# Score maxima as float16 pairs before the transpose, and value sums that start with a product instead of a zero matmul: one layer kernel on Trainium2

## Chip, cores and metric

One core of a Trainium2 chip. The metric is the device time in microseconds of one execution of the whole kernel; the number compared is the median of several executions. The kernel before has a median of 2942.72 us in 3 runs (2941.49 to 2947.78).

## The reference

One transformer layer over 2048 latent tokens (width 1024) with 256 context tokens: a modulated RMS norm, one input projection, a bidirectional chunked retention (4 heads), a grouped-query attention (8 query heads of 64, 2 key heads, 256 + 2048 keys), an output projection and a squared-ReLU MLP. The change sits in the attention:

```python
def _dense_attention(q, k, v):
    s = jnp.einsum('bqkgd,bskd->bkgqs', q, k).astype(jnp.float32) * ATT_SCALE
    p = jax.nn.softmax(s, axis=-1).astype(v.dtype)
    return jnp.einsum('bkgqs,bskd->bqkgd', p, v)
```

Everything is float32 in the reference. The kernel reaches that with pairs of float16: a `hi` part (the value cast down) and a `lo` part (what the cast lost).

## The kernel before

The kernel runs in three stages one behind another: projections (up to about 655 us), attention with retention and output projection beside it (about 655 to 1660 us), and the MLP (to the end).

**Groups and steps.** The attention is cut into 32 *groups*, one for each of 16 tiles of 128 queries and 2 key heads; a group holds 4 query heads, so 512 query columns. There are NK = 18 tiles of 128 keys. A table of events, `on(k, phase, fn)`, says which function issues its instructions in step k; within a step the phases run in the order `begin, scores, piece, maximum, early, exp, cast, low, chain, pe, values, late, dma`. `chain` is a list from which one entry is taken after the phases maximum, low and late. The order that results is the program order of each engine; no engine reorders. A group takes 18 steps, and a group's maxima are computed beside the exponentials of the group before.

**Maxima (lines 160 to 196).** For each group, 18 `piece` matmuls (L165, L169) give scores with the query on the partitions, in PSUM tiles `mp`, of which there are two buffers; `maximum` (L178, VectorE) reduces each piece to a negated maximum in `nm`. `least` (L184) takes the minimum over a head's five numbers and writes it twice, by two reductions, into columns 64 and 96 of a float32 tile `mt` (column 80 holds a constant). `turn` (L189, TensorE) transposes `mt` by four float32 matmuls with the identity, into a PSUM tile that is the next `mp` buffer. `rows` (L192, ScalarE) copies rows 64 to 127 of it, divided by 8192, into the float16 query tile `qr`, and `rows2` (L196, VectorE) overwrites rows 96 to 127 with what that cast lost. So the maxima become extra rows of the queries, and the score matmuls (L202, L203) subtract them.

**Exponentials and values.** `exp` (L208, ScalarE) writes float32 probabilities, `cast` (L212, ScalarE) their float16 `phi`, `low` their `plo`, on GpSimd (L219) for five of nine pairs of key tiles and on VectorE (L221) for the others. `values` (L223 to 236) adds, for each pair of key tiles, 16 products into two PSUM tiles `o`: a `plo` product (65 columns wide) and a `phi` product (129 columns) for each of 2 key tiles and 4 heads. Two heads share one `o` tile. Ahead of a group's first pair, two matmuls of a zero tile with 258 columns (L227) open the sums of the two tiles with `start=True`.

**Beside it.** Retention (L1083 to 1155), the output projection (L1259 to 1281) and the norm ahead of the MLP (L1288 to 1316) are spread over the same steps and use all engines; L1233, L1226 and L1231 prepare output weights in the first groups.

Of the kernel before, what the change touches and what calls it, by code (L numbers as in the profile page):

```python
# [11 lines left out]
F32 = mybir.dt.float32  # L12
F32R = mybir.dt.float32r
F16 = mybir.dt.float16
BF16 = mybir.dt.bfloat16
I32 = mybir.dt.int32
AF = mybir.ActivationFunctionType
ALU = mybir.AluOpType
AX = mybir.AxisListType
# [3 lines left out]
P = 128  # L23
# [6 lines left out]
NK = NT + NC  # L30
H = 4
CH = 128
HD = 64
# [3 lines left out]
PSHIFT = 8  # L37

ROW = 8192.0
VW = 2 * HD + 1  # L40
# [14 lines left out]
def layer_kernel(ctx: ExitStack, tc: tile.TileContext, a: dict, out: bass.AP):  # L55
    nc = tc.nc
    mm = nc.tensor.matmul

    const = ctx.enter_context(tc.tile_pool(name="const", bufs=1, reuse_waits="tile"))
    dram = ctx.enter_context(tc.tile_pool(name="dram", bufs=1, space=DRAM))  # L60

    ident = const.tile([P, P], F32, name="ident")
    make_identity(nc, ident)

    def split(hi, lo, src, eng=None):
        nc.scalar.activation(hi, src, AF.Copy)
# [67 lines left out]
    wv = kp.tile([P, 2, NK, VW + 1], F16, name="wv")  # L134
# [6 lines left out]
    class Group:  # L141
# [36 lines left out]
            nc.vector.tensor_reduce(dst, src, axis=AX.X, op=ALU.max, negate=True)  # L178

        def least(self, mt):  # L180
            self.mt = mt
            nm = self.nm.rearrange("p a b c -> p (a b) c")
            for c in (64, 96):
                nc.vector.tensor_reduce(mt[:, :, c], nm, axis=AX.X, op=ALU.min)  # L184

        def turn(self):
            self.m = psS.tile([P, 4, P], F32, name="mp", tag="mp")
            for h in range(4):
                nc.tensor.transpose(self.m[:, h], self.mt[:, h], ident)  # L189

        def rows(self):
            nc.scalar.activation(self.qr[64:, 1], self.m[64:], AF.Copy, scale=1 / ROW)  # L192

        def rows2(self):
            lo = self.qr[96:, 1]
            nc.vector.scalar_tensor_tensor(lo, self.m[96:], 1 / ROW, lo, op0=ALU.mult, op1=ALU.subtract)  # L196

        def scores(self, kt):
            ps = self.s[kt] = psS.tile([P, 512], F32, name="st", tag="st")
# [23 lines left out]
        def values(self, j):  # L223
            if j == 0:
                self.o = [psV.tile([P, 2, VW], F32, name=f"o{b}", tag=f"o{b}") for b in range(2)]
                for o in self.o:
                    mm(o, zeros, wv[:, 0, :2, :VW], start=True, stop=False)  # L227
            hi, lo = self.hi.pop(j), self.lo.pop(j)
            for i in range(2):
                v = wv[:, self.g, 2 * j + i]  # L230
                for h in range(4):
                    o = self.o[h // 2][:, h % 2]
                    c = slice(h * P, (h + 1) * P)
                    last = 2 * j + i == NK - 1 and h % 2 == 1
                    mm(o[:, : HD + 1], lo[:, i, c], v[:, : HD + 1], start=False, stop=False)  # L235
                    mm(o, hi[:, i, c], v[:, :VW], start=False, stop=last)  # L236

        def evacuate(self):
            self.so = op.tile([P, 4, VW], F32, name="so", tag="so")
# [20 lines left out]
    with ExitStack() as st:  # L260
# [5 lines left out]
        op = st.enter_context(tc.tile_pool(name="op", bufs=2, reuse_waits="tile"))  # L266
        sm = st.enter_context(tc.tile_pool(name="sm", bufs=3, reuse_waits="tile"))
# [623 lines left out]
        for n, (g, c) in enumerate(todo):  # L891
# [7 lines left out]
            last = c == len(PLAN[g]) - 1  # L899
# [10 lines left out]
            for m, (kind, i) in enumerate(GROUPS[g]):  # L910
                if not (kind == "c" and col in (C_RQ, C_RG, C_AQ)):
                    ps, k = (begun.pop(m), 6) if n == 0 and m in begun else (None, 4)
# [40 lines left out]
    op = pool(attn, "op2", 2)  # L953
# [13 lines left out]
    nc.vector.tensor_tensor(unit, ident[:, 64:65], ident[:, 96:97], op=ALU.add)  # L967
    nc.vector.tensor_tensor(unit, unit, ident[:, 80:81], op=ALU.add)
    nc.vector.tensor_scalar_mul(unit, unit, ROW)
    zeros = vp.tile([P, P], F16, name="zeros")  # L970
    nc.vector.memset(zeros, 0.0)
    mts = [vp.tile([P, 4, P], F32, name=f"mt{i}") for i in range(2)]
    for mt in mts:
        nc.gpsimd.memset(mt, 0.0)

        nc.gpsimd.memset(mt[:, :, 80], PSHIFT * math.log(2.0) * HD**0.5)

    def more_keys(g, i):
        s = slice(i * 768, (i + 1) * 768)
# [8 lines left out]
    def on(k, phase, fn, *args):  # L988
        events.setdefault((k, phase), []).append((fn, args))
# [28 lines left out]
    def attention():  # L1018
        for n, g in enumerate(groups):
            k = NK * n  # L1020
            if n > 0:
                on(k - 14, "dma", g.load)
                on(k - 1, "late", g.minima, sm)
                for i in range(NK):
                    on(k + i, "piece", g.piece, i)
                    on(k + i + 1, "maximum", g.maximum, i)
            else:
                on(k + NK, "begin", g.load)
            on(k + NK, "chain", g.least, mts[n % 2])
            on(k + NK + 1, "piece", g.turn)  # L1030
            on(k + NK + 2, "cast", g.rows)
            on(k + NK + 3, "early", g.rows2)
            k += LAG
            for i in range(NK):
                on(k + i, "scores", g.scores, i)
                on(k + i + 1, "exp", g.exp, i)
            for j in range(NK // 2):
                on(k + 2 * j + 3, "cast", g.cast, j)
                if j in POOL_PAIRS:
                    on(k + 2 * j + 4, "low", g.low, j)  # L1040
                else:
                    for i in range(2):
                        on(k + 2 * j + 4 + i, "low", g.low, j, i)
                on(k + 2 * j + 6, "values", g.values, j)
            k += NK + 5
            on(k, "cast", g.evacuate)
            on(k + 1, "chain", g.invert)
            on(k + 2, "late", g.combine, ats)
        return NK * len(groups) + LAG + 8
# [758 lines left out]
```

## Time and profile before

| | |
|---|---|
| median of 3 runs | 2942.72 us (2941.49 to 2947.78) |
| the profiled execution's own time | 2946.76 us |
| its span, first to last instruction | 2945.0 us |
| granted TensorE clock, mean | 0.987 |
| TensorE / VectorE / ScalarE / GpSimd busy | 94% / 74% / 47% / 53% of the span |
| first and last transposition of maxima (L189) | 678.2 and 1604.3 us |

In the profile PE is TensorE's matmuls, PEld its weight loads, DVE is VectorE, ACT ScalarE, POOL GpSimd, SP the queue that issues DMAs. A matmul's end is modelled: matmuls overlap, so a matmul's cost to the queue is read from the distance between the starts of two neighbours, not from its duration. The same holds in small for DVE, where an instruction may start a little ahead of the end of the one before. A wait is put down to what came last.

### The profile page before, as it was taken

The page shows a single profiled execution, that of the slowest core. Times are in us where ns is not written, and L with a number is a line of the kernel's source. Part 1 is how long each engine was busy: PE and PEld are TensorE (multiplying, and loading weights), DVE is VectorE, ACT ScalarE, POOL GpSimd, SP SyncE. Part 2 cuts the span into 40 slices and gives each one's busy share as a digit, 9 for nine tenths or more (in the row PEclk, how much of TensorE's full clock was granted, in tenths as well). Part 3 has the DMA queues.
Part 4 walks back from the last instruction along what each step waited for, and adds up shares of the span by engine and source line. Part 5 has one row for each costly group of instructions (what it writes and reads, how often), then busy time and mean ns, then how long its engine had stood idle before and what let it go on. Part 6 is the DMA issues. An engine that isn't in the chain of part 4 may idle for free. (4 is left out here: it accounts for less than half of the span.)

```text
span 2945.0 us, 45295 instructions
## 1 busy us (share of the span) xinstructions
PE 2776.2 (94%) x17140; PEld 1648.8 (56%) x17140; DVE 2181.6 (74%) x3330; ACT 1388.0 (47%) x2280; POOL 1550.2 (53%) x1274
## 2 busy tenths in 40 slices
PE   7998898998799999999999899999999899999998
PEld 3777677775566666565666444444444344444443
DVE  5889847647987777777876577778777777777776
ACT  2333323325777777787777433333332333333332
POOL 3536326425876667887656656664443444444332
PEclk9999999999999999999999999999999999999999
DMA  9988843426412123332211723331114511111111
GB/s 300 340 283 280 271 154 107 160 67 201 137 46 81 49 63 121 90 104 85 73 63 51 273 92 101 104 102 60 53 51 154 173 60 47 54 51 51 58 44 58
DMA packets 265305, 346.95 MB, mean 118 GB/s; under 512 B 106231, under 2 KB 163831, under 8 KB 263294
## 3 DMA queue, kind: packets, MB, share of 16 engines
q1 hardware_dynamic: 254806, 336.57, 35.2%
q10 hardware_dynamic: 10280, 7.48, 0.9%
q8 instruction: 135, 2.21, 0.3%
q14 instruction: 84, 0.69, 0.1%
HBM read 272.52 MB, written 71.46 MB: 117 GB/s over the span
## 5 line engine op out<-in xcount | busy, mean ns | idle before, releaser
L178 DVE TENSOR_REDUCE nm<-mp 128x1 f32<-128x512 f32 (+1 forms) x576 | 390.9, 685 | 172.6 <-PE mp L165 143.3
L219 POOL TENSOR_TENSOR plo<-p,phi 128x1024 f16<-128x1024 f32 x160 | 353.7, 2212 | 172.9 <-ACT phi L212 139.6
L208 ACT ACTIVATE p<-st 128x512 f32<-128x512 f32 x576 | 338.1, 597 | 188.5 <-PE st L203 118.7
L1582 PE MATMUL pd<-w2hi,uhi 128*128 128x512 f16 x1024 | 388.0, 379 | 12.9 <-DVE acc L1585 12.6
L1583 PE MATMUL pd<-w2lo,uhi 128*128 128x512 f16 x1024 | 388.0, 379 | 0.6 <-DVE w2lo L71 0.6
L1584 PE MATMUL pd<-w2hi,ulo 128*128 128x512 f16 x1024 | 388.1, 379 | 0.0
L1585 DVE SCALAR_TENSOR_TENSOR acc<-pd,sc,acc 128x512 f32<-128x512 f32 x512 | 366.4, 739 | 5.7 <-PE pd L1584 5.6
L1522 PE MATMUL pu<-hf,w1f 128*128 128x512 f16 x896 | 340.1, 380 | 2.5 <-DVE q L1545 2.0
L1523 PE MATMUL pu<-hf,w1f 128*128 128x512 f16 x896 | 340.0, 379 | 0.0
L1524 PE MATMUL pu<-hf,w1f 128*128 128x512 f16 x896 | 339.8, 379 | 0.0
L824 PE MATMUL pso<-whi,hi_l 128*128 128x512 f32 (+1 forms) x768 | 295.8, 388 | 10.2 <-ACT xs L524 4.3
L212 ACT ACTIVATE phi<-p 128x1024 f16<-128x1024 f32 x288 | 303.8, 1055 | 0.0
L826 PE MATMUL pso<-whi,lo_l 128*128 128x512 f32 (+1 forms) x768 | 293.7, 383 | 4.1 <-DVE lo_l L67 4.1
L825 PE MATMUL pso<-wlo,hi_l 128*128 128x512 f32 (+1 forms) x768 | 292.9, 382 | 0.8 <-DVE wlo L67 0.7
L235 PE MATMUL o<-wv,plo 128*128 128x65 f16 x2304 | 235.9, 193 | 23.9 <-POOL plo L219 17.0
L221 DVE TENSOR_TENSOR plo<-p,phi 128x512 f16<-128x512 f32 x256 | 240.9, 942 | 18.6 <-ACT phi L212 15.7
L236 PE MATMUL o<-wv,phi 128*128 128x129 f16 x2304 | 243.8, 221 | 0.0
L235 PEld LDWEIGHTS <-plo 128*128 128x128 f16 x2304 | 206.7, 98 | 59.8 <-POOL plo L219 25.9
L202 PE MATMUL st<-qr,ks 128*128 128x512 f16 x576 | 220.2, 382 | 12.4 <-ACT p L208 10.4
L1534 POOL TENSOR_TENSOR r<-r 128x512 f32<-128x512 f32 x64 | 66.3, 1039 | 295.2 <-ACT r L1533 295.2
L203 PE MATMUL st<-qr,ks 128*128 128x512 f16 x576 | 220.0, 382 | 0.1
L165 PE MATMUL mp<-ks,qr 128*128 128x512 f16 x512 | 196.7, 384 | 23.0 <-DVE nm L178 22.2
(324 smaller groups left out, 5751.4 us busy)
## 6 DMA issues: line engine op xcount, KB each, us to landing
wm<-in_w_ff SPq DMA_DIRECT2D x64, 512.0 KB, 5.3
w1r<-in_w_ff SPq DMA_DIRECT2D x64, 512.0 KB, 4.6
ws<-in_w_ff SPq DMA_DIRECT2D x124, 256.0 KB, 3.5
wst<-in_w_in SPq DMA_DIRECT2D x60, 512.0 KB, 5.5
wst<-in_w_mod SPq DMA_DIRECT2D x32, 512.0 KB, 6.0
hf<-hp SPq DMA_DIRECT2D x56, 256.0 KB, 3.2
hf<-hf SPq DMA_DIRECT2D x14, 1024.0 KB, 7.1
orv<-rv SPq DMA_DIRECT2D x35, 256.0 KB, 4.0
```

The lines of the kernel that those rows point to most:

```text
L178: nc.vector.tensor_reduce(dst, src, axis=AX.X, op=ALU.max, negate=True)
L208: nc.scalar.activation(self.p[kt // 2][:, kt % 2], self.s.pop(kt), AF.Exp, scale=HD**-0.5)
L212: nc.scalar.activation(hi, self.p[j], AF.Copy)
L219: nc.gpsimd.tensor_tensor(lo, p, hi, op=ALU.subtract)
L235: mm(o[:, : HD + 1], lo[:, i, c], v[:, : HD + 1], start=False, stop=False)
L1522: mm(pu[i], whi, hi, start=k == 0, stop=False)
L1523: mm(pu[i], whi, lo, start=False, stop=False)
L1524: mm(pu[i], wlo, hi, start=False, stop=k == 3)
L1582: mm(ps, uh, wh, start=f == 0, stop=False)
L1583: mm(ps, uh, wl, start=False, stop=False)
L1584: mm(ps, ul, wh, start=False, stop=f == NF - 1)
L1585: nc.vector.scalar_tensor_tensor(acc[:, c], ps, sc2, acc[:, c], op0=ALU.mult, op1=ALU.add)
```

## The change

`least` reduces once into a small float32 tile, multiplies it by 1/8192 into float16 column 64, and computes the rest, `m/8192 - hi`, into float16 column 96; each of the three reads what the one before wrote. `mt` is float16, the constant of column 80 is divided by 8192 too, and `turn` is four float16 matmuls with a float16 identity (made once, at the start). `rows` copies without a scale, and `rows2` is gone. `least` moves from the phase `chain` to the phase `maximum` of the same step (`begin` for the first group), so ahead of `low`. In `values`, the zero tile and its two matmuls are gone; for a group's first key tile the `phi` product comes ahead of the `plo` product, and the first head of each `o` tile has `start=True`.

```diff
+    ident16 = const.tile([P, P], F16, name="ident16")
+    nc.vector.tensor_copy(ident16, ident)
...
         def least(self, mt):
             self.mt = mt
+            m = sm.tile([P, 4], F32, name="least", tag="least")
             nm = self.nm.rearrange("p a b c -> p (a b) c")
-            for c in (64, 96):
-                nc.vector.tensor_reduce(mt[:, :, c], nm, axis=AX.X, op=ALU.min)
+            nc.vector.tensor_reduce(m, nm, axis=AX.X, op=ALU.min)
+            nc.vector.tensor_scalar_mul(mt[:, :, 64], m, 1 / ROW)
+            nc.vector.scalar_tensor_tensor(
+                mt[:, :, 96], m, 1 / ROW, mt[:, :, 64], op0=ALU.mult, op1=ALU.subtract
+            )
 
         def turn(self):
             self.m = psS.tile([P, 4, P], F32, name="mp", tag="mp")
             for h in range(4):
-                nc.tensor.transpose(self.m[:, h], self.mt[:, h], ident)
+                mm(self.m[:, h], self.mt[:, h], ident16, start=True, stop=True)
 
         def rows(self):
-            nc.scalar.activation(self.qr[64:, 1], self.m[64:], AF.Copy, scale=1 / ROW)
-
-        def rows2(self):
-            lo = self.qr[96:, 1]
-            nc.vector.scalar_tensor_tensor(lo, self.m[96:], 1 / ROW, lo, op0=ALU.mult, op1=ALU.subtract)
+            nc.scalar.activation(self.qr[64:, 1], self.m[64:], AF.Copy)
...
                 self.o = [psV.tile([P, 2, VW], F32, name=f"o{b}", tag=f"o{b}") for b in range(2)]
-                for o in self.o:
-                    mm(o, zeros, wv[:, 0, :2, :VW], start=True, stop=False)
...
+                    first = j == i == 0
+
+                    if first:
+                        mm(o, hi[:, i, c], v[:, :VW], start=h % 2 == 0, stop=False)
                     mm(o[:, : HD + 1], lo[:, i, c], v[:, : HD + 1], start=False, stop=False)
-                    mm(o, hi[:, i, c], v[:, :VW], start=False, stop=last)
+                    if not first:
+                        mm(o, hi[:, i, c], v[:, :VW], start=False, stop=last)
...
-    zeros = vp.tile([P, P], F16, name="zeros")
-    nc.vector.memset(zeros, 0.0)
-    mts = [vp.tile([P, 4, P], F32, name=f"mt{i}") for i in range(2)]
+    mts = [vp.tile([P, 4, P], F16, name=f"mt{i}") for i in range(2)]
...
-        nc.gpsimd.memset(mt[:, :, 80], PSHIFT * math.log(2.0) * HD**0.5)
+        nc.gpsimd.memset(mt[:, :, 80], PSHIFT * math.log(2.0) * HD**0.5 / ROW)
...
-            on(k + NK, "chain", g.least, mts[n % 2])
+            on(k + NK, "maximum" if n else "begin", g.least, mts[n % 2])
             on(k + NK + 1, "piece", g.turn)
             on(k + NK + 2, "cast", g.rows)
-            on(k + NK + 3, "early", g.rows2)
```

What follows is the program order at three places, an instruction a row, with the semaphores that it waits for by the engine that raises them. Line numbers are those of each kernel: `maximum` is L178 before and L180 after, `low` on VectorE L221 and L224, `piece` L165 and L167, the score matmuls L202/L203 and L205/L206; `ks_6523` and `ks_6525` are the second key tile `ks2`.

VectorE at the end of the seventh group's maxima, before:

```order
L178 TENSOR_REDUCE nm<-mp 128x2 [waits PE_49]
L221 TENSOR_TENSOR plo<-p_9071,phi 128x512 [waits DVE_49,Activation_49,Pool_49]
L184 TENSOR_REDUCE mt_6530<-nm 128x4 [waits DVE_49]
L184 TENSOR_REDUCE mt_6530<-nm 128x4
L178 TENSOR_REDUCE nm<-mp 128x1 [waits PE_49]
L221 TENSOR_TENSOR plo<-p_9071,phi 128x512
L178 TENSOR_REDUCE nm<-mp 128x1 [waits PE_49] x2
L196 SCALAR_TENSOR_TENSOR qr<-mp,qr 32x512 [waits Activation_49]
```

The same place after:

```order
L180 TENSOR_REDUCE nm<-mp 128x2 [waits PE_49]
L187 TENSOR_REDUCE least<-nm 128x4 [waits DVE_49]
L188 TENSOR_SCALAR mt_6530<-least 128x4 [waits DVE_49]
L189 SCALAR_TENSOR_TENSOR mt_6530<-least,mt_6530 128x4 [waits DVE_49]
L224 TENSOR_TENSOR plo<-p_9065,phi 128x512 [waits Activation_49,Pool_49]
L180 TENSOR_REDUCE nm<-mp 128x1 [waits PE_49]
L224 TENSOR_TENSOR plo<-p_9065,phi 128x512
L180 TENSOR_REDUCE nm<-mp 128x1 [waits PE_49] x2
```

The two reductions behind the `low` became three instructions ahead of it, each of which waits for VectorE itself, and the 32x512 instruction four rows further on is gone.

TensorE at the same group's transposition, before; the two L165 rows are the second and third piece of the next group:

```order
L189 MATMUL mp<-ident,mt_6530 128x128 [waits DVE_49,PE_49]
L189 MATMUL mp<-ident,mt_6530 128x128 x3
L165 LDWEIGHTS qr
L165 MATMUL mp<-ks,qr 128x512 [waits DVE_49]
...
L202 LDWEIGHTS ks
L202 MATMUL st<-qr,ks 128x512 [waits Activation_49]
L203 LDWEIGHTS ks_6523
L203 MATMUL st<-qr,ks_6523 128x512
L165 LDWEIGHTS qr
L165 MATMUL mp<-ks,qr 128x512 [waits DVE_49]
```

The same place after:

```order
L196 LDWEIGHTS mt_6530 [waits DVE_49]
L196 MATMUL mp<-ident_65,mt_6530 128x128 [waits PE_49]
...
L196 LDWEIGHTS mt_6530
L196 MATMUL mp<-ident_65,mt_6530 128x128
L167 LDWEIGHTS qr
L167 MATMUL mp<-ks,qr 128x512 [waits DVE_49]
...
L206 LDWEIGHTS ks_6525
L206 MATMUL st<-qr,ks_6525 128x512
L167 LDWEIGHTS qr
L167 MATMUL mp<-ks,qr 128x512 [waits Activation_49]
```

The four transposing matmuls have weight loads of their own, and the third piece of the next group waits for ScalarE instead of VectorE: it takes the buffer of the transposed maxima, which `rows` frees, where before it took the second piece's buffer, which `maximum` frees.

TensorE at the first values of a later group, before:

```order
L227 LDWEIGHTS zeros
L227 MATMUL o_9380<-wv,zeros 128x258 [waits Activation_49]
L227 LDWEIGHTS zeros
L227 MATMUL o_9381<-wv,zeros 128x258 [waits Activation_49]
L235 LDWEIGHTS plo [waits Pool_49]
L235 MATMUL o_9380<-wv,plo 128x65
L236 LDWEIGHTS phi
L236 MATMUL o_9380<-wv,phi 128x129
```

The same place after:

```order
L239 LDWEIGHTS phi
L239 MATMUL o_9375<-wv,phi 128x129 [waits Activation_49]
L240 LDWEIGHTS plo [waits Pool_49]
L240 MATMUL o_9375<-wv,plo 128x65
L239 LDWEIGHTS phi
L239 MATMUL o_9375<-wv,phi 128x129
```

The two zero matmuls are gone, and the first product needs only the `phi` part. On the other engines and in the DMA queue the order is the same in both kernels, apart from the cast that makes the float16 identity near the start.

## Prediction, made before the changed kernel ran

> **What bounds the kernel now.** The page first, for the whole; then the busy time by stretches of the attention, since the change touches nothing else.
>
> ```profile
> span 2945.0 us, 45295 instructions
> PE 2776.2 (94%) x17140; PEld 1648.8 (56%) x17140; DVE 2181.6 (74%) x3330; ACT 1388.0 (47%) x2280; POOL 1550.2 (53%) x1274
> ```
>
> ```profile
> 700.00:820.00 120.00, 96.41 (x929) 67.82 (x928) 107.81 (x199) 84.00 (x135) 92.20 (x62) 0.97 0.54 170
> 820.00:1120.00 300.00, 287.58 (x2697) 190.69 (x2695) 237.74 (x426) 227.23 (x370) 193.44 (x143) 1.00 0.20 63
> 1120.00:1360.00 240.00, 219.14 (x2011) 143.07 (x2010) 186.49 (x309) 183.29 (x305) 199.38 (x151) 0.99 0.37 109
> 1360.00:1600.00 240.00, 230.53 (x2141) 149.69 (x2139) 186.34 (x336) 180.46 (x292) 149.88 (x114) 1.00 0.18 58
> ```
>
> The columns are the stretch, its length, and the busy time of PE, PEld, DVE, ACT and POOL. There are three regimes. From 820 to 1120 and from 1360 to 1600 PE is busy 96% and the bound. From 700 to 820 DVE has 107.8 of 120 (90%) and PE 80%: DVE leads. From 1120 to 1360 PE has 91% and POOL 83%: mixed. The waits say the same. These are who waited for whom, in total us, times, and longest: in the first PE-bound stretch DVE waits for PE, in the first stretch PE waits for DVE, in the mixed one PE waits for POOL.
>
> ```profile
> DVE nm L178 <- PE mp L165: 43.2, 57, 1.7
> ```
>
> ```profile
> PE mp L165 <- DVE nm L178: 14.2, 14, 2.0
> ```
>
> ```profile
> PE o L235 <- POOL plo L219: 10.7, 7, 2.5
> ```
>
> The 32 transpositions lie 29.9 us apart (678.2 to 1604.2): 4 in the first stretch, 10, 8 and 8 in the others, and one at either end. The sum below goes by these stretches.
>
> **The change on PE.** How often, from the views of the two source lines; what each costs the queue, from starts in the timeline.
>
> ```profile
> L227 PE MATMUL o<-wv,zeros x64: 272/274/274, 691.4 to 1615.8; 128*128 128x258 f16 x64
> ```
>
> ```profile
> L189 PE MATMUL mp<-ident,mt x128: 272/273/476, 678.2 to 1604.3; 128*128 128x128 f32 x128
> ```
>
> ```profile
> 921.81 0.60 PE L189 MATMUL mp<-ident,mt 128*128 128x128 f32 x4
> 922.24 0.38 PE L165 MATMUL mp<-ks,qr 128*128 128x512 f16 x1
> ...
> 993.16 0.39 PE L227 MATMUL o<-wv,zeros 128*128 128x258 f16 x2
> 993.38 0.19 PE L235 MATMUL o<-wv,plo 128*128 128x65 f16 x1
> 993.41 0.22 PE L236 MATMUL o<-wv,phi 128*128 128x129 f16 x1
> 993.47 0.19 PE L235 MATMUL o<-wv,plo 128*128 128x65 f16 x1
> ```
>
> - Zero matmuls: two per group, 993.38 - 993.16 = 0.22 us. They go whole, since the `phi` and `plo` products are as many as before. Nothing covers them: the `plo` product behind them starts at once, so it was not waiting.
> - Transposition: four float32 matmuls take 922.24 - 921.81 = 0.43 us. The trace has no float16 matmul of 128 columns from a 128-column weight with its own load but L236, with 129 columns, at 993.47 - 993.41 = 0.06. Bounds: 0.03 each (L235, 65 columns) and the old 0.11 each, so a saving of 0.31 down to 0 per group. I take 0.055 each, L236 being all but the same instruction: 0.22 for four, 0.21 saved.
>
> Together 0.43 us a group, 13.8 us over 32 groups. What of it comes through depends on the regime. In the 18 groups of the PE-bound stretches 7.7, of which I take the 96% that PE is busy: **-7.4**. In the 8 mixed groups 3.4, of which half, since there PE's starts are released by POOL as often as by PE's own queue: **-1.7**. In the 4 DVE-led groups nothing. The two groups at the ends: **-0.4**.
>
> **The change on DVE.** First what goes, then what comes.
>
> ```profile
> 861.77 0.68 DVE L221 TENSOR_TENSOR plo<-p,phi 128x512 f16<-128x512 f32 x1
> 862.37 0.25 DVE L184 TENSOR_REDUCE mt<-nm 128x4 f32<-128x20 f32 x2
> 862.53 0.68 DVE L178 TENSOR_REDUCE nm<-mp 128x1 f32<-128x512 f32 x1
> ...
> 1402.70 0.68 DVE L178 TENSOR_REDUCE nm<-mp 128x1 f32<-128x512 f32 x1
> 1403.42 0.70 DVE L196 SCALAR_TENSOR_TENSOR qr<-mp,qr 32x512 f16<-32x512 f32 x1
> 1404.15 0.69 DVE L1311 TENSOR_TENSOR u<-bank,a 128x512 f32<-128x512 f32 x1
> ```
>
> ```profile
> 659.78 0.15 DVE L968 TENSOR_TENSOR unit<-unit,ident 128x1 f32<-128x1 f32 x1
> 659.97 0.15 DVE L969 TENSOR_SCALAR unit<-unit 128x1 f32<-128x1 f32 x1
> ```
>
> A 0.68 us instruction is followed after 0.60 (861.77 to 862.37): the next starts 0.08 before its end. The two reductions hold the queue 862.53 - 862.37 = 0.16. Around L196 the starts are 1402.70 and 1404.15, 1.45 apart, where 0.60 would do: it costs 0.85. So 1.01 us goes. L969 reads what L968 wrote and starts 0.04 *after* its end (0.19 behind its start): that is the price of a dependent start. The three new ones all depend on the one before: the first starts 0.03 after the maximum's end instead of 0.08 before (0.11 late), then 0.17 + 0.03 (a reduction's 0.17), 0.15 + 0.03, and 0.15 less 0.08 for what follows: 0.56. DVE gains 0.45 a group, bounds 0.2 (each step 0.08 more) and 0.76 (no dependent start costs).
>
> [...]
>
> Where DVE waits for PE (18 groups) this gain is hidden. In the 4 DVE-led groups it counts: **-1.8**.
>
> `least` ahead of `low` makes `mt` ready 0.57 us after the last maximum's end, against 0.77 now (-0.08 + 0.60 + 0.08 + 0.17), and the next group's first maximum 0.40 later. In PE-bound groups there is room: the tile written at 862.37 is ready at 862.62, and PE takes it at 864.03, behind work of its own:
>
> ```profile
> 864.03 0.60 PE L189 MATMUL mp<-ident,mt 128*128 128x128 f32 x4
> ```
>
> **The wait at the third piece.** Here is DVE, PE and ACT two steps on.
>
> ```profile
> 980.05 0.69 DVE L178 TENSOR_REDUCE nm<-mp 128x1 f32<-128x512 f32 x1 [0.42 <-PE mp L165]
> 980.30 0.59 ACT L192 ACTIVATE qr<-mp 64x512 f16<-64x512 f32 x1
> 980.79 0.38 PE L165 MATMUL mp<-ks,qr 128*128 128x512 f16 x1 [0.35 <-DVE nm L178]
> ```
>
> The third piece reuses the second's buffer and waits for its maximum (980.74). After the change, by the program order, it mostly waits for `rows`, which ends at 980.89 here. In this group that would be no better; the order keeps DVE for this group and 8 others. Where matmuls of the output projection stand between (L1274 to L1276 in the order above the prediction), PE comes later than both. Behind the third piece on PE stand the next values, and ACT and DVE wait for those no sooner than two steps on. A gain of 0.1 us in a third of the groups, bounds +0.5 and -0.5 each: **-0.7** in all, most of it in DVE-led groups, whose waits above are at this piece.
>
> **The port.** This is the one cost that can grow.
>
> ```profile
> 1332.12 1.11 DVE L1295 TENSOR_TENSOR ss<-ss 128x1 f32<-128x1 f32 x1
> ```
>
> ```profile
> 1331.61 1.60 POOL L71 TENSOR_TENSOR hp<-hb,hp 128x512 f16<-128x512 f32 x1
> ```
>
> ```profile
> L1295 DVE TENSOR_TENSOR ss<-ss x14: 130/160/1114, 869.2 to 1614.8; 128x1 f32<-128x1 f32 x14
> ```
>
> ```profile
> 706.72 2.49 POOL L219 TENSOR_TENSOR plo<-p,phi 128x1024 f16<-128x1024 f32 x1 [0.93 <-ACT phi L212]
> ...
> 863.92 2.13 POOL L219 TENSOR_TENSOR plo<-p,phi 128x1024 f16<-128x1024 f32 x1 [2.21 <-ACT phi L212]
> ...
> 1571.02 2.13 POOL L219 TENSOR_TENSOR plo<-p,phi 128x1024 f16<-128x1024 f32 x1
> ```
>
> L1295 does one element from two SBUF tiles in 0.16 us, but 1.11 when POOL runs: it ends 0.02 after POOL does (1333.23 against 1333.21). The new third instruction has two SBUF tiles too. L184 has one and L196 reads PSUM; neither shows this. In PE-bound groups POOL waits for ACT at that place (the 863.92 row: idle 2.21 us before, from 861.71). Counted group by group, POOL runs at that place in 13 of 31 groups (first and last: the 706.72 and 1571.02 rows), 9 of them in the first and the mixed stretch; but there L221, which has the same two inputs, already pays now. I charge one `plo` on POOL (2.13) in the group at 706.72, where POOL starts just as the chain would and DVE leads, and nothing elsewhere: **+2.2**.
>
> **Sum.** -7.4 - 1.7 - 0.4 - 1.8 - 0.7 + 2.2 = -9.8. The profiled execution took 2946.76 us (span 2945.0 and 1.76 around it), so 2937.0 on its own scale. It lies 4.0 above the median of the runs, 2942.72, to which I carry the difference: **2933 us**.
>
> **Rivals.**
> - *No change:* the freed PE time turns into waiting for `plo` and `p`, because the loop from score through ACT and POOL back to PE sets the pace. For it: DVE, ACT and POOL are 62 to 83% busy. Against: in 820 to 1120 DVE waits 43.2 us for PE, and only 4% of PE is idle. If a quarter of the PE gain survives: -2.4 - 1.8 + 2.2 = -2.0, 2941 us.
> - *Slower, by the port:* POOL runs a two-input operation behind another, and takes the port between the second and third new instruction, and again ahead of `low`. Place: the groups in which POOL runs where `least` now stands, 13 by their rows. Price: two more `plo` of 2.13 each, 4.3 x 13 = 55 us of DVE at most; half on the path gives +28 - 9.8 - 2.2, 2959 us. It decides from six of those groups on (6 x 4.3 = 26, half on the path 13, against the 12.0 gained without the port). Against: L1295 got in as soon as POOL ended, so DVE wins a hand-over. [...]
> - *The transposition saves nothing* (float16 with its own weight load at 0.11 each): 6.8 less on PE, of which 4.5 on the path: 2937.5 us. The 0.06 of L236 speaks against it.
>
> **Chances and range.** Forecast 0.68, saves-nothing transposition 0.07, no change 0.15, slower 0.10. The forecast's own range: the full 13.8 with -1.8 and -2 at the third piece and no port, 2925; half the PE gain, nothing from DVE or the third piece, and the port, 2940. To leave out no more than 2 in 10 the range reaches over no change: 2925 to 2943. A measurement of this kernel can tell 0.2% (5.9 us), so faster means below 2936.8: nine tenths of the forecast and half the third rival, 0.65; within 0.2% (to 2948.6) the rest of these and no change, 0.25; slower 0.10.
>
> **What would show it.** The page after: 64 fewer L227, four float16 transpositions 0.22 us apart from start to start of the next, no 32x512 on DVE. Right, if the way from the first to the last transposition (678.2 to 1604.3) shrinks by about 9 us, most of it in the PE-bound groups, with PE there still at 96%. Wrong, if PE's share there falls (no change), or if the third new instruction's median is far above 0.16 us and its end follows POOL's (the port), or if the third piece's wait for ACT grows beyond the 0.35 above.

## The result, and the profile after

The change makes the kernel slower: 2961.24 us median in 4 runs (2956.95 to 2964.78) against 2943.89 in 4 runs of the kernel before (2941.49 to 2947.78), a ratio of 1.0057 with a 95% interval of 1.0039 to 1.0075. The forecast was 2933. The profiled run took 2961.19 us. Its page, span and busy line:

```profile
span 2959.4 us, 45118 instructions
PE 2770.3 (94%) x17076; PEld 1642.0 (55%) x17076; DVE 2189.0 (74%) x3330; ACT 1387.9 (47%) x2280; POOL 1549.0 (52%) x1274
```

PE has 5.9 us less to do than before, as meant; DVE has 7.4 more, though a 0.7 us instruction a group is gone; the span is 14.4 longer. The same four stretches of the attention (columns as in the prediction, the granted clock behind POOL):

```profile
700.00:820.00 120.00, 96.18 (x913) 68.70 (x913) 104.47 (x192) 81.69 (x132) 90.44 (x62) 0.93 0.50 160
820.00:1120.00 300.00, 281.39 (x2639) 184.40 (x2636) 236.97 (x416) 224.94 (x367) 188.29 (x141) 0.99 0.20 63
1120.00:1360.00 240.00, 214.26 (x1944) 137.52 (x1943) 186.41 (x305) 179.18 (x298) 197.71 (x149) 0.97 0.37 105
1360.00:1600.00 240.00, 222.43 (x2075) 145.32 (x2074) 188.77 (x329) 176.63 (x286) 144.32 (x109) 0.99 0.19 62
```

In every stretch PE does fewer instructions in the same time (2697 became 2639, 2141 became 2075; two a group, 20 and 16 there, are the missing zero matmuls), and in the second and fourth its share falls from 96% to 94 and 93%, the sign that the prediction named for being wrong. A cleaner cut is the way from the first to the last transposition, one row for each kernel. Before:

```profile
678.20:1604.30 926.10, 856.56 (x7942) 566.03 (x7943) 740.52 (x1304) 693.98 (x1132) 645.38 (x474) 0.99 0.29 89
```

After:

```profile
675.80:1615.70 939.90, 851.54 (x7881) 559.67 (x7881) 751.20 (x1304) 693.32 (x1132) 642.18 (x474) 0.98 0.28 88
```

The way is 13.8 us longer. PE's busy time fell by 5.0 only, where 0.43 us in 31 groups makes 13.3, because more of it ran at a lower clock. An estimate from the traces, which takes half of PE's busy time in the stretches at half the clock as lost, gives 9.6 us lost before and 19.0 in the change, so 14.4 less work at full clock. PE's idle time on the way rose from 69.5 to 88.4. So the 13.8 us are 18.9 of waiting and 9.4 of lower clock, less the 14.4 saved, and the view of waits says for whom PE waits. PE's longest waits in the attention (675 to 1620), before:

```profile
PE mp L165 <- DVE nm L178: 22.2, 36, 2.0
PE o L235 <- POOL plo L219: 16.0, 12, 2.5
PE st L202 <- ACT p L208: 10.4, 18, 1.5
PE o L235 <- DVE plo L221: 6.7, 14, 1.0
```

After:

```profile
PE mp L167 <- DVE nm L180: 32.1, 34, 3.6
PE o L240 <- POOL plo L222: 16.0, 13, 2.9
PE st L205 <- ACT p L211: 9.8, 15, 1.8
PE o L240 <- DVE plo L224: 9.3, 16, 1.3
```

The pieces' wait for VectorE's maxima grew by 9.9 us. It grew at the second piece of the next group, which stands right behind the transposition: 2.0 us in 4 groups before, 15.3 in 12 after. What VectorE does there stands in the views of the new lines (shortest, median and longest in ns; below a line, who waited for it):

```profile
L188 DVE TENSOR_SCALAR mt<-least x32: 176/178/2014, 657.5 to 1613.8; 128x4 f16<-128x4 f32 x32
...
L189 DVE SCALAR_TENSOR_TENSOR mt<-least,mt x32: 176/178/1197, 657.7 to 1614.0; 128x4 f16<-128x4 f32 x32
...
  PEld L196: 5.6, 8
  PE mp L196: 2.7, 2
```

Four elements take 0.18 us, and up to 2.01. One such place, VectorE, GpSimd and the transposition around 1341 (the "..." leave out other engines and rows):

```profile
1339.00 2.13 POOL L222 TENSOR_TENSOR plo<-p,phi 128x1024 f16<-128x1024 f32 x1
...
1340.32 0.17 DVE L187 TENSOR_REDUCE least<-nm 128x4 f32<-128x20 f32 x1
...
1340.53 0.63 DVE L188 TENSOR_SCALAR mt<-least 128x4 f16<-128x4 f32 x1
1341.09 1.28 POOL L1110 TENSOR_TENSOR oqb<-oqt,tb 128x512 f32<-128x512 f32 x1
...
1341.20 1.20 DVE L189 SCALAR_TENSOR_TENSOR mt<-least,mt 128x4 f16<-128x4 f32 x1
...
1342.31 1.72 DVE L224 TENSOR_TENSOR plo<-p,phi 128x512 f16<-128x512 f32 x1
1342.32 1.15 POOL L73 TENSOR_TENSOR hp<-hs,hp 128x512 f16<-128x512 f32 x1
1342.45 0.40 PE L196 MATMUL mp<-ident,mt 128*128 128x128 f16 x4
...
1343.95 0.68 DVE L180 TENSOR_REDUCE nm<-mp 128x1 f32<-128x512 f32 x1
...
1344.68 0.46 PE L167 MATMUL mp<-ks,qr 128*128 128x512 f16 x1 [1.83 <-DVE nm L180]
```

Read the ends. L222 ends at 1341.13 and L188 at 1341.16. GpSimd's next operation is in by then, ends at 1342.37, and L189 ends at 1342.40. Then L73 ends at 1343.47, and L224, which needs 0.69 us alone, ends at 1344.03. Three VectorE operations, one behind another, are each held up by one GpSimd operation; the next maximum comes at 1343.95, and the piece on PE that needs it has idled 1.83 us. In the whole trace 17 of the 64 new operations are longer than 0.25 us, 11 of L188 and 6 of L189, in 12 groups (in 5 both); together they wait 13.1 us, and each of the 17 ends 0.03 to 0.04 us behind the end of a GpSimd operation.

### The profile page after: what moved, and what is told of

It is laid out like the page before. It is cut to its first block, busy times and chain, and to the rows that moved or that the text cites. A ratio compares the mean times of both kernels' runs of the same rounds, so it can differ in the third digit from the quotient of the medians.

```text
span 2959.4 us, 45118 instructions
## 1 busy us (share of the span) xinstructions
PE 2770.3 (94%) x17076; PEld 1642.0 (55%) x17076; DVE 2189.0 (74%) x3330; ACT 1387.9 (47%) x2280; POOL 1549.0 (52%) x1274
## 5 line engine op out<-in xcount | busy, mean ns | idle before, releaser
L180 DVE TENSOR_REDUCE nm<-mp 128x1 f32<-128x512 f32 (+1 forms) x576 | 390.2, 684 | 171.9 <-PE mp L167 143.4
L222 POOL TENSOR_TENSOR plo<-p,phi 128x1024 f16<-128x1024 f32 x160 | 352.6, 2204 | 174.1 <-ACT phi L215 145.9
L1585 PE MATMUL pd<-w2hi,uhi 128*128 128x512 f16 x1024 | 388.0, 379 | 12.6 <-DVE acc L1588 12.4
L224 DVE TENSOR_TENSOR plo<-p,phi 128x512 f16<-128x512 f32 x256 | 251.0, 982 | 21.5 <-ACT phi L215 21.3
L242 PE MATMUL o<-wv,phi 128*128 128x129 f16 x2176 | 236.3, 222 | 0.0
L205 PE MATMUL st<-qr,ks 128*128 128x512 f16 x576 | 221.5, 385 | 11.3 <-ACT p L211 11.0
L167 PE MATMUL mp<-ks,qr 128*128 128x512 f16 x512 | 197.9, 387 | 34.4 <-DVE nm L180 32.1
L206 PE MATMUL st<-qr,ks 128*128 128x512 f16 x576 | 221.8, 385 | 0.0
```

The source lines that it names most:

```text
L222: nc.gpsimd.tensor_tensor(lo, p, hi, op=ALU.subtract)
L1585: mm(ps, uh, wh, start=f == 0, stop=False)
```

## The experiments

Medians are those of the run's own comparison; the kernel before had 2946.68, 2948.08 and 2948.19 us (23, 23 and 17 runs) beside the three sets of four. "Way" is the length from first to last transposition, as above. Way and busy times are of one profiled execution each; executions of one kernel differ by several us (the kernel before 2941.63 to 2952.29 us in the third set), so a difference of a few us in these columns shows nothing by itself.

| kernel | median us | ratio, 95% interval | way us | PE busy | DVE busy |
|---|---|---|---|---|---|
| before | 2943.89 | 1 | 926.1 | 856.6 | 740.5 |
| the change | 2961.24 | 1.0057 [1.0039, 1.0075] | 939.9 | 851.5 | 751.2 |
| e1 values only | 2945.90 | 0.9998 [0.9988, 1.0008] | 925.9 | 851.0 | 744.6 |
| e2 maxima only | 2961.73 | 1.0045 [1.0031, 1.0059] | 940.9 | 855.2 | 749.0 |
| e3 change, `least` behind `low` | 2966.59 | 1.0063 [1.0050, 1.0076] | 947.3 | 848.9 | 758.4 |
| e4 before, `least` ahead | 2953.23 | 1.0023 [1.0013, 1.0032] | 936.1 | 859.4 | 748.1 |
| e5 four reductions ahead | 2950.05 | 1.0002 [0.9994, 1.0011] | 924.7 | 842.7 | 740.3 |
| e6 four reductions behind | 2945.70 | 0.9997 [0.9987, 1.0007] | 923.3 | 844.8 | 736.9 |
| e7 one reduction behind | 2937.68 | 0.9962 [0.9950, 0.9974] | 914.3 | 839.1 | 725.7 |
| e8 before, pair added | 2971.15 | 1.0078 [1.0065, 1.0092] | 953.6 | 865.3 | 771.5 |
| e9 reduction and multiplication | 2949.48 | 1.0004 [0.9995, 1.0013] | 925.8 | 843.5 | 744.7 |
| e10 one reduction, float32 | 2937.58 | 0.9968 [0.9957, 0.9979] | 917.1 | 852.9 | 722.6 |
| e11 one reduction ahead | 2938.78 | 0.9972 [0.9960, 0.9983] | 915.5 | 839.8 | 724.7 |
| e12 one reduction, zeros kept | 2933.78 | 0.9954 [0.9941, 0.9966] | 912.1 | 842.8 | 720.3 |

The first four runs ask which part of the change costs: the values' new order, the maxima's three operations, or their place ahead of `low`. The expectations of that set name theories by letters. What they and the prediction call the port is seen in the traces as a VectorE operation that takes longer and ends 0.03 to 0.04 us behind a GpSimd operation (the 17 above); that the two engines share a port was not shown.

**e1_values_only.** The kernel before with the second half of the change alone: no zero matmuls, the first key tile's `phi` product opens the sums.

```diff
-                for o in self.o:
-                    mm(o, zeros, wv[:, 0, :2, :VW], start=True, stop=False)
...
+                    if first:
+                        mm(o, hi[:, i, c], v[:, :VW], start=h % 2 == 0, stop=False)
...
```

> The kernel before with the change to the value sums alone (no zero matmuls, first product opens the sum). Theory A (the maxima's chain of three on VectorE, its waits at the port shared with GpSimd and the halved TensorE clock behind the stalls cost the time; the values' part is pure gain): 0.22 us in each of 32 groups less on TensorE, so -4 to -7 us against before. Theory B (opening a sum with the phi product costs something of its own): at least +8 us.

It brings nothing (0.9998), and the interval leaves out both expectations. PE's busy time on the way fell by 5.6 us and the way by 0.2. PE's waits in the attention show where the rest went:

```profile
PE o L237 <- POOL plo L219: 17.3, 13, 2.5
PE st L202 <- ACT p L208: 13.7, 19, 1.9
PE o L237 <- DVE plo L221: 8.7, 15, 1.3
```

Against the rows of before these are 1.3, 3.3 and 2.0 more: 6.6 us, which is 0.21 in 31 groups. By these rows the zero matmuls had been run in time in which PE would have waited a moment later anyway.

**e2_maxima_only.** The change with the zero matmuls and the old order of the values.

```diff
+                for o in self.o:
+                    mm(o, zeros, wv[:, 0, :2, :VW], start=True, stop=False)
...
```

> The changed kernel with the value sums of before (zero matmuls kept). Theory A: the loss of the whole change plus what the zero matmuls cost, +17 to +25 us against before, with the same blocked multiplications (1 to 2 us) in about 10 groups. Theory B: -3 us or better against before.

1.0045 against the change's 1.0057, with intervals that overlap: the loss is in the maxima. By the medians it is 15 us, a little under the 17 to 25 of theory A. 19 of its 64 new operations are long, 14.6 us of waiting.

**e3_least_behind_low.** The change with `least` back in the phase behind `low`.

```diff
-            on(k + NK, "maximum" if n else "begin", g.least, mts[n % 2])
+            on(k + NK, "chain" if n else "begin", g.least, mts[n % 2])
```

> The changed kernel with the three operations put back behind low (phase chain of the same step). Theory A with the port as the main thing: the two new operations still meet GpSimd, and the time stays at +10 us or more against before. Theory C (the place: 0.4 us more on VectorE ahead of low makes low lose its turn to GpSimd): -4 us or better against before.

Slower than before all the same (1.0063), so the place is not the cause by itself. 20 operations are long here, 20.8 us of waiting, and now the transposition stands right behind them. L189 and who waited for it:

```profile
L189 DVE SCALAR_TENSOR_TENSOR mt<-least,mt x32: 176/178/2047, 657.7 to 1620.4; 128x4 f16<-128x4 f32 x32
...
  PEld L196: 24.3, 17
  PE mp L196: 16.5, 14
```

**e4_old_least_ahead.** The kernel before with its two reductions moved ahead of `low`, nothing else.

```diff
-            on(k + NK, "chain", g.least, mts[n % 2])
+            on(k + NK, "maximum" if n else "begin", g.least, mts[n % 2])
```

> The kernel before with its two reductions moved ahead of low (phase maximum), nothing else. [...] Theory A: within 3 us of before. Theory C in its strong form (anything ahead of low costs): +8 us or more.

6.6 us slower, between the two expectations, though no operation was added and the reductions never take over 0.18 us; `low` comes 0.16 us later. In the trace four groups are 2.0 to 3.3 us longer (the second, third, 16th and 28th); the other 27 together are 0.4 us shorter. The 28th shows one way in which that happens. Before, the second `low` starts 0.02 us ahead of GpSimd's operation, and it is GpSimd's that takes longer:

```profile
1489.13 0.69 DVE L221 TENSOR_TENSOR plo<-p,phi 128x512 f16<-128x512 f32 x1
1489.15 2.65 POOL L219 TENSOR_TENSOR plo<-p,phi 128x1024 f16<-128x1024 f32 x1 [4.34 <-ACT phi L212]
```

In e4 GpSimd's starts 0.11 us ahead, and `low` takes 2.57 us:

```profile
1496.83 2.13 POOL L219 TENSOR_TENSOR plo<-p,phi 128x1024 f16<-128x1024 f32 x1 [4.34 <-ACT phi L212]
1496.94 2.57 DVE L221 TENSOR_TENSOR plo<-p,phi 128x512 f16<-128x512 f32 x1
```

In the 16th it is the same (a `low` of 2.21 us behind GpSimd's, of 1.00 ahead of it before). In the second and third groups together 5.1 us more than before go at half the clock, 1.7 of which the fourth gets back.

After these runs two theories were left. *P*: the multiplication (L188) and the combining operation (L189) wait for GpSimd (they take up to 2.01 us in the change). *L*: it is the length of what stands around `low` that costs, whatever the operations are.

**e5_reductions_ahead.** The change with L188 and L189 made of reductions: the same two parts, four operations instead of three, in the same place (the scale of 1/8192 goes back to ScalarE's copy).

```diff
-            m = sm.tile([P, 4], F32, name="least", tag="least")
+            x = sm.tile([P, 4, 2], F32, name="least", tag="least")
...
-            nc.vector.tensor_reduce(m, nm, axis=AX.X, op=ALU.min)
-            nc.vector.tensor_scalar_mul(mt[:, :, 64], m, 1 / ROW)
-            nc.vector.scalar_tensor_tensor(
-                mt[:, :, 96], m, 1 / ROW, mt[:, :, 64], op0=ALU.mult, op1=ALU.subtract
-            )
+            nc.vector.tensor_reduce(mt[:, :, 64], nm, axis=AX.X, op=ALU.min)
+            nc.vector.tensor_reduce(x[:, :, 0], nm, axis=AX.X, op=ALU.min)
+            nc.vector.tensor_reduce(x[:, :, 1], mt[:, :, 64:65], axis=AX.X, op=ALU.min, negate=True)
+            with nc.allow_low_precision(reason="a remainder"):
+                nc.vector.tensor_reduce(mt[:, :, 96], x, axis=AX.X, op=ALU.add)
...
```

> The change with its multiplication and its combining operation replaced by reductions (four in place of three operations, so the work ahead of the low parts gets about 0.17 us longer a group, by the 174 to 178 ns of the rows), all of kinds that waited for GpSimd in no row so far. Theory P (the two operations wait for GpSimd at the port, up to 2.0 us each): the waits go, what is left is the shift of the low parts, which cost 6.6 us for 0.16 us in the run with the old reductions ahead: 2950 to 2958, no row of these lines over 0.3 us. Theory L (the length of the work ahead of the low parts alone sets the loss): not better than the change, 2960 to 2970.

2950.05, ratio 1.0002 against the change's 1.0057: 11 us less by the medians, 16 by the ratios. The four lines:

```profile
L187 DVE TENSOR_REDUCE mt<-nm x32: 180/180/183, 658.7 to 1598.8; 128x4 f16<-128x20 f32 x32
...
L188 DVE TENSOR_REDUCE least<-nm x32: 162/164/166, 658.8 to 1598.9; 128x4 f32<-128x20 f32 x32
...
L189 DVE TENSOR_REDUCE least<-mt x32: 158/159/161, 658.9 to 1599.0; 128x4 f32<-128x4 f16 x32
...
L191 DVE TENSOR_REDUCE mt<-least x32: 172/173/176, 659.1 to 1599.2; 128x4 f16<-128x8 f32 x32
```

128 operations, and the longest is 183 ns. The place and the length are those of the change. One group here, the last maximum and the start of `low` behind the four:

```profile
1335.49 0.69 DVE L180 TENSOR_REDUCE nm<-mp 128x2 f32<-128x512 f32 x1 [1.66 <-PE mp L171]
...
1336.70 0.88 DVE L224 TENSOR_TENSOR plo<-p,phi 128x512 f16<-128x512 f32 x1
```

One group of the change in which nothing blocks:

```profile
972.45 0.69 DVE L180 TENSOR_REDUCE nm<-mp 128x2 f32<-128x512 f32 x1 [1.31 <-PE mp L171]
...
973.67 0.69 DVE L224 TENSOR_TENSOR plo<-p,phi 128x512 f16<-128x512 f32 x1
```

From the maximum's end to the start of `low` it is 0.52 us here (1336.18 to 1336.70) and 0.53 in the change (973.14 to 973.67). GpSimd works at this place in e5 too (an operation of 1.28 us from 1335.76 on), and none of the four is held up. So P holds for this part of the loss. It is the small operations that make it: all `low` on VectorE together take 242.6 us of the way in e5, 241.7 in the change and 231.0 before, so `low` waits as long without the two operations as with them.

**e6_reductions_behind.** The same, with `least` behind `low`.

```diff
-            on(k + NK, "maximum" if n else "begin", g.least, mts[n % 2])
+            on(k + NK, "chain" if n else "begin", g.least, mts[n % 2])
```

> The same four reductions put back behind the low parts, where the kernel before had its two. Theory P: neither the port nor the shift is left, the low parts start as before; the turns wait a little longer for the maxima (0.35 us later than the two old reductions), PE gains 0.43 us a group where it bounds: 2938 to 2946. Theory L: the same place as before, so also about 2946, but no better. If the run with three operations behind the low parts (2966) was slow because of the length of its chain and not of the port, this one is as slow: 2960 or more.

2945.7, as before (0.9997), and some 20 us better than e3 (1.0063), which differs from it only in the operations that make the two parts (three of them, or four reductions and the scale on ScalarE). With reductions in their place, ahead of `low` or behind it, the change is therefore worth nothing to within 0.13%.

**e7_hi_only_behind.** The change with one reduction straight to float16, behind `low`; the second part of the maxima is left out, and the scale is on ScalarE as in e5.

```diff
-            m = sm.tile([P, 4], F32, name="least", tag="least")
...
-            nc.vector.tensor_reduce(m, nm, axis=AX.X, op=ALU.min)
-            nc.vector.tensor_scalar_mul(mt[:, :, 64], m, 1 / ROW)
-            nc.vector.scalar_tensor_tensor(
-                mt[:, :, 96], m, 1 / ROW, mt[:, :, 64], op0=ALU.mult, op1=ALU.subtract
-            )
+            nc.vector.tensor_reduce(mt[:, :, 64], nm, axis=AX.X, op=ALU.min)
...
-            on(k + NK, "maximum" if n else "begin", g.least, mts[n % 2])
+            on(k + NK, "chain" if n else "begin", g.least, mts[n % 2])
```

> The change with one reduction straight to float16, behind the low parts, and no second part: the low part of the maxima is left out, so part of the computation is. It has the whole gain of PE and takes 0.16 us and more from VectorE in each group: the most that float16 transposes can bring in this schedule. If PE bounds the groups: 2933 to 2938. If, as the run with the values alone showed, PE's gain turns into waits for ScalarE's exponentials and VectorE: 2941 to 2946.

2937.68, 0.9962: faster than both kernels. The number fits the first of the two expectations; e10 shows that the reason given there (PE bounds) does not.

**e8_added_pair_ahead.** The kernel before, with a multiplication and a combining operation more in 31 groups, whose results nothing reads.

```diff
+    def dummy_pair(g):
+        m = g.nm.rearrange("p a b c -> p (a b) c")[:, :, 0]
+        d = [sm.tile([P, 4], F16, name=f"dm{i}", tag=f"dm{i}") for i in range(2)]
+        nc.vector.tensor_scalar_mul(d[0], m, 1 / ROW)
+        nc.vector.scalar_tensor_tensor(d[1], m, 1 / ROW, d[0], op0=ALU.mult, op1=ALU.subtract)
...
+            if n:
+                on(k + NK, "maximum", dummy_pair, g)
```

> The kernel before with nothing changed but two operations added ahead of the low parts in 31 groups: a multiplication and a combining operation of the change's kinds and sizes, whose results nothing reads. PE keeps its whole work. Theory P: they wait for GpSimd at the port in some ten groups as in the change, and low loses its turn: 2958 to 2970. Theory L (0.36 us more ahead of the low parts, by the 6.6 us that 0.16 cost): 2955 to 2962, rows of the two operations at 0.18 us. A third, that the loss sits in the float16 transposes or the turn's later wait: 2946 to 2950.

2971.15, 1.0078: two operations of 0.16 us, read by nobody, cost 23 us. It lies just above P's range and far above L's. The lines:

```profile
L1021 DVE TENSOR_SCALAR dm<-nm x31: 153/160/2040, 705.0 to 1627.0; 128x4 f16<-128x4 f32 x31
```

```profile
L1022 DVE SCALAR_TENSOR_TENSOR dm<-nm,dm x31: 161/164/2130, 705.2 to 1627.2; 128x4 f16<-128x4 f32 x31
```

18 of them are long, by 16.2 us, and each of these ends up to 0.03 us behind the end of a GpSimd operation. 62 instructions more on DVE made its time on the way 30.9 us more and the way 27.5.

**e9_multiplied_hi_behind.** e7 with its one reduction made two operations, a float32 reduction and a multiplication into float16, which takes the scale over from ScalarE.

```diff
+            m = sm.tile([P, 4], F32, name="least", tag="least")
...
-            nc.vector.tensor_reduce(mt[:, :, 64], nm, axis=AX.X, op=ALU.min)
+            nc.vector.tensor_reduce(m, nm, axis=AX.X, op=ALU.min)
+            nc.vector.tensor_scalar_mul(mt[:, :, 64], m, 1 / ROW)
...
```

> The run with one reduction straight to float16 (2937.7), with that one operation made two: a float32 reduction and a multiplication into float16, behind the low parts; no second part of the maxima in either. Theory P: the multiplication waits for GpSimd in some ten groups, by 0.3 to 2 us, which the turns wait for: 2945 to 2954. Theory L (length alone, 0.18 us more behind the low parts): 2938 to 2940.

2949.48, 12 us worse than e7, in the middle of P's range. The multiplication alone waits for GpSimd, in 11 groups, 10.4 us together:

```profile
L188 DVE TENSOR_SCALAR mt<-least x32: 175/177/1897, 656.2 to 1597.8; 128x4 f16<-128x4 f32 x32
```

**e10_hi_only_float32.** The kernel before without the second part: one reduction, no `rows2`, float32 transpositions and zero matmuls as they were.

```diff
-            for c in (64, 96):
-                nc.vector.tensor_reduce(mt[:, :, c], nm, axis=AX.X, op=ALU.min)
+            nc.vector.tensor_reduce(mt[:, :, 64], nm, axis=AX.X, op=ALU.min)
...
-            on(k + NK + 3, "early", g.rows2)
```

> The kernel before with its second part of the maxima left out: one float32 reduction, float32 transposes, the zero products, and no combining operation for the low row. It tells what of the 10 us of the run with one float16 reduction came from VectorE's dropped work (0.16 us and 0.85 us a group) and what from PE's. If PE's shorter work brings it: 2944 to 2949, as before. If VectorE's dropped work brings it: 2936 to 2941. In between, 2940 to 2944, if each has a share.

2937.58, the same as e7: VectorE's dropped work brings as much without one PE instruction less. In the trace of before nothing waited for the dropped L196, so by that trace it is VectorE's time and not a shorter chain that counts.

**e11_hi_only_ahead.** e7 with its reduction ahead of `low`.

```diff
-            on(k + NK, "chain" if n else "begin", g.least, mts[n % 2])
+            on(k + NK, "maximum" if n else "begin", g.least, mts[n % 2])
```

> The run with one float16 reduction (2937.7), with that reduction ahead of the low parts. By the 6.6 us that 0.16 us ahead of them cost in the kernel before: 2942 to 2946. If that loss hung on the particular rhythm of that kernel and not on the place: 2934 to 2940.

2938.78, against 2937.68: the place costs nothing that can be told here. So the 6.6 us of e4 are no price of the place as such; as its rows show, it matters which engine happens to be first where `low` and a GpSimd operation meet.

**e12_hi_only_zeros.** e7 with the zero matmuls and the old order of the values.

```diff
+                for o in self.o:
+                    mm(o, zeros, wv[:, 0, :2, :VW], start=True, stop=False)
...
```

> The run with one float16 reduction (2937.7), with the zero products put back ahead of the values, so that only the maxima differ from before. By the run with the values alone, which brought nothing: 2936 to 2940. If the values' 0.22 us a group counts once VectorE's work is out of the way: 2941 to 2945.

2933.78, 0.9954, the best of all, below both expectations. Against e7 the zeros add 3.8 us of PE's time and the way is 2.2 shorter: PE's idle time is 69.3 against 75.2. The intervals of the two ratios overlap, so that the zeros help is not shown; that they cost nothing is, by this run as by e1. A softmax divides by a sum taken with the same shift, so a maximum rounded to float16, being the same for all keys of a query, cancels; by that argument e12 may stand for the kernel, as far as the shifted exponentials stay in range, which no run here tests.

## Why the prediction was wrong

The forecast was 9.8 us less, 12.0 without the 2.2 charged for the port; by the ratio the change is 16.8 us slower. e5, which has no blocked operation, is 0.6 slower. So 12.6 us of the miss are a gain that did not come, and 14.0 are the waits for GpSimd (2.2 charged, 16.2 measured), each within the few us of the intervals.

- **What bounds the attention** is the step that failed first. "96% busy" was read as "PE is the bound", and 0.43 us a group was carried through at that share. In the table the way does not follow PE's busy time: e1 takes 5.6 us from it and the way keeps its length, and e5 takes 13.9 from it, with DVE as busy as before, and the way is 1.4 shorter. It goes with DVE's, in which the time that GpSimd holds an operation up counts as busy: taking 18.0 us from DVE alone (e10) takes 9.0 from the way, adding 30.9 to it alone (e8) adds 27.5. PE, at 92% of the way, waits 69.5 us in it before, and its waits for DVE, GpSimd and ScalarE fill up with what it is spared.
- **Zero matmuls, 0.22 a group.** The size held; "nothing covers them" did not. e1 brings back 6.6 us as waits for `plo` and `p`, the first rival's mechanism (no change, 2941, 0.15), which fits this half of the change; e5 and e6 fit it for the whole, with the waits for GpSimd away.
- **Transpositions, 0.21 a group.** Held: 0.43 became 0.22 us for four. In the change:

```profile
975.32 0.39 PE L196 MATMUL mp<-ident,mt 128*128 128x128 f16 x4
...
975.54 0.38 PE L167 MATMUL mp<-ks,qr 128*128 128x512 f16 x1
```

  So the third rival, which put the float16 transpositions at 0.11 each, falls. What the saving is worth in time is not shown: e12, which has it, is 3.8 us below e10 by the medians, of 6.5 that 31 groups make, but the intervals of the two ratios overlap.
- **The chain on DVE** was put at 0.56 us of the queue. Where nothing blocks it is 0.61: `low` starts 0.53 behind the maximum's end instead of 0.08 before it. In the change L188 and L189 start 0.03 to 0.04 us behind the end of the operation that they read (one L188, 0.11), as the row of L969 told; the second and third operation are 0.18 and not 0.15.
- **The port** was the mis-sized term: one GpSimd operation of 2.13, +2.2 in all. Measured: 17 operations in 12 groups, 13.1 us on VectorE, and e5, which has none, is 11 to 16 us faster. Three parts of the step failed. First, only the third operation was charged, since "neither shows this" was said of a reduction and of an operation that reads PSUM; a multiplication from SBUF to SBUF had no row, and 11 of the 17 waits are its. In the rows here L188, the multiplication, takes up to 2014 ns in the change, and no reduction of e5 more than 183 ns. Second, "DVE wins a hand-over": at 1341 GpSimd's next operation was in (1341.09) before the dependent L189 came (1341.20). Third, the groups where GpSimd runs at that place were counted (13) and then set aside because `low` waited there already; at 1341 it waits again, behind the two. (In sum `low` waits as long in e5; what the change adds is the waits of the small operations. No run shows that the two share a port.) The sign that the prediction named, a median far above 0.16 us, was the wrong one to look at: the medians are 0.18, and six ends of the third operation follow GpSimd's.
- **The second rival** (slower by the port, 2959) had the waits for GpSimd: 12 groups against its 13 and its threshold of six. That its time is near too (2959 against 2961) is partly luck: it charged 4.3 us a group, where the operations wait 1.1 (13.1 in 12 groups), and put half of that on the path, where 13.1 us cost 11 to 16. It was given 0.10.
- **The third piece** was to wait mostly for `rows`. In the traces it waited for VectorE's maximum in 14 groups before (10.7 us), and after it in 7 (8.4 us) and for `rows` in 4 (1.5 us): 0.8 us less, by one execution each, near the 0.7 forecast. The prediction did not look at the second piece, whose wait grew by 13.3 us, since VectorE is late. (A gain of 0.1 us in a third of the groups would be 1.0 and not 0.7; and without dependent starts the prediction's numbers give a gain of 0.78, not 0.76. Neither slip changes the outcome.)
- **The clock** was left out. It is part of the loss: on the way the granted clock falls from 0.99 to 0.98, 9.4 us of PE's time by the estimate above. The last section has when it falls.

What stays open: which share of the 17 us would be left at full clock, since a long wait can bring both (e3 loses 20 us with only 2.9 us more of PE's time at the lower clock, so the waits alone can cost as much); and why all `low` together take 11 us more of the way in e5 and in the change than before.

## What to carry to other kernels

A busy share of 96% says that an engine has little slack, not that time taken from it shortens the stretch: look at what it would wait for next, and try the cheapest edit that takes work from one engine alone. Here the kind of a small VectorE operation counted and not its size: beside GpSimd four elements took up to 2.01 us through a multiplication (L188 in the change) and up to 2.13 through a two-input operation (L1022 in e8), and at most 0.18 through a reduction (e5). The change's two operations one behind another gave GpSimd two places to get in: 11 waits at the first, 6 at the second, in 5 groups both. In e4 a shift of 0.16 us went with another order of the two engines: in its 28th group `low` took 2.57 us instead of 0.69, and GpSimd's operation 2.13 instead of 2.65. Whether other kernels show the same is to be read from their traces.

## What the runs showed of the hardware

In the change PE's granted clock fell to 0.50 behind waits of 2.18 us (until 978.53) and 1.83 us (until 1344.68). The windows of 3.41 us around these two and a third, in which PE's longest wait is 1.02 us (PE's busy time is the first column behind the length, the granted clock stands behind POOL):

```profile
976.19:979.60 3.41, 1.23 (x19) 0.89 (x18) 3.01 (x4) 2.81 (x6) 2.02 (x4) 1.00 0.67 207
979.60:983.01 3.41, 3.41 (x22) 1.95 (x20) 1.42 (x3) 1.91 (x3) 3.41 (x3) 0.50 0.31 81
```

```profile
1341.44:1344.85 3.41, 1.58 (x22) 0.93 (x19) 3.41 (x4) 2.34 (x4) 3.41 (x3) 1.00 0.06 13
1344.85:1348.26 3.41, 2.18 (x8) 1.25 (x7) 2.73 (x4) 1.54 (x2) 3.41 (x3) 0.50 0.59 125
1402.88:1406.29 3.41, 1.65 (x23) 1.03 (x22) 3.31 (x6) 2.98 (x5) 3.41 (x4) 1.00 0.00 0
1406.29:1409.70 3.41, 2.35 (x16) 1.65 (x15) 3.41 (x5) 0.25 (x1) 2.31 (x1) 1.00 0.00 0
```

A window with PE busy for 1.23 or 1.58 of 3.41 us is followed by one at half the clock, one with 1.65 is not. The half-clock stretches of a trace all start on one grid of 3.41 us (14 of them before, 19 in the change). In the fourteen traces (700 to 1700 us) 71 of the 72 windows on that grid with PE busy for 42% or less were followed by half the clock (the other, in e1, had 41.5%); of the 43 between 42 and 49%, ten were; from 49% up, of more than 3800 that themselves ran at the full clock, one was (in e9, 52%); before and the change alone have 13 of 13, 3 of 4 and none of 550. An estimate from these windows: a single wait of 2 us inside one leaves PE at most 1.41 of 3.41 us (41%) and by the counts costs up to 1.7 us more, half of a window at half the clock; split evenly between two it leaves 71% in each and by the counts costs nothing more. In the 31 groups the time lost in this way (half of each stretch at half the clock) is 10.4 us before, 20.5 in the change and 3.5 in e12.
